# Earlier squares of x, square root for the norm factors, and three moved steps in a one-core encoder layer

## The chip, the cores and the metric

The kernel runs on one core of one Trainium2 chip. The core's engines are TensorE (PE, matmuls; PEld its weight loads), VectorE (DVE), ScalarE (ACT), GpSimd (POOL) and SyncE (SP, which issues most of the transfers). The metric is the device time of one execution in microseconds. Three executions of the kernel before took 2711.42 to 2716.16 us, with a median of 2714.16.

## The reference

One layer of a hybrid encoder for 512 tokens of width 2048, in float32:

```python
h = rmsnorm(x, mix_norm)
proj = h @ w_mix_in                       # 2048 -> 4*1024 + 16 + 3*1024
y_gdn = gdn_group(proj, ...)              # 8 heads x 128: gated delta rule
y_sc = shortconv_group(proj, ...)         # gated short convolution
x = x + concat(y_gdn, y_sc) @ w_mix_out
x = x + memory_xattn(rmsnorm(x), rmsnorm(mem), w_q, w_k, w_v, w_o)   # 256 memory tokens, 4 heads
x = x + conv_ffn(rmsnorm(x), w_ffn_up, ffn_conv, w_ffn_down)         # 2048 -> 2*5632 -> 2048
return rmsnorm(x, final_norm)
```

An `rmsnorm` multiplies each token by the reciprocal square root of the mean of its squares. The gates of the delta rule (`b_raw`, `a_raw`) are 16 columns of the input projection. Within a chunk the delta rule solves a unit lower triangular system per head, which the kernel does by inverting diagonal blocks of 32 x 32.

## The kernel before, in words

Activations lie with features on the 128 partitions and tokens along the row, so x is 16 tiles of 128 x 512. Each float32 weight piece (128 x 1024, 512 KB) is loaded by `wpiece` (line 136, tile `wst`, five buffers), rounded by ACT to `whi`, and the rest `wlo` is taken by DVE (lines 146 and 147). Both have three buffers, so the splits run up to three pieces ahead of PE.

The stages follow one another:

1. `values` (line 340): v of the memory tokens, before any norm of x is there. Eight column pairs n2 = 0 to 7; for each, 2 x 2 pieces go through `proj`, and `mem_out` (line 329) takes the result from PSUM by ACT and DVE (`kt`, `kth`; lines 332 to 337). The pairs 0 to 2 are held until `mem_norm` (after pair 2), so six `mem_out` calls come together then, and two after each later pair.
2. Beside it x is prepared. `load_x` loads tiles of x (SP, line 381), `square_x` calls `add_squares` (lines 260 to 264): ACT squares a tile into a tile `sq`, POOL adds it to `xacc`. `rstd_rows` (line 250) sums `xacc` over the partitions by a matmul with ones (`psn`, line 255), and `rsqrt` (line 228) makes the factor: Ln and Exp with scale -0.5 on ACT, then one Newton step on DVE (lines 241 to 243). `norm_x` (line 394) then scales the tiles of x by that factor and the gain. `beside_values` says behind which pair each of these stands.
3. A stage that folds v into the output weights (`psmo`, lines 634 to 636); in it x's operands for the input projection are made, and the 16 gate columns (`wba`, loaded at line 409) are multiplied with x (line 426).
4. The input projection with seven block products per quad (`quad_left`, `quad_right`; tiles `px`, `py`, `pz`).
5. The memory's keys (`psk`, line 1015), their fold into the queries' weights (`pswk`, lines 1032 to 1036) and the first half of the output rows (`out_row`, tile `psx1`). Into this PE work the delta rule is woven: generators `prepare_chunk`, `invert`, `solve`, `recur`, `scaled` for two groups of four heads (hb = 0, 1). `place` and `tick` count a clock of PE work in the code; a generator that has yielded (cost, wait) goes on when that clock has passed its wait. `invert` (lines 866, 867) is the substitution: 31 dependent steps of two DVE operations each, with a yield after each fourth. `solve` (line 876) then brings the inverted blocks (`xd`) and `v` back from DRAM and starts with transposes on PE. The last generator stores the heads' result to `y_d` (line 982), which the second half of the output rows reads.
6. Scores, softmax and the attention's output rows (`psx2`): `x1` is loaded from `x1_d` (line 1182), the product is added (line 1183), squares go to `acc2` by `add_squares`, and the sum is transposed for later (line 1159). `out_piece` loads and splits the next weights.
7. The feed-forward part: up projection with quads as in 4 (the norm's factor `r2` is made beside the first of them, by `norm_rows`), convolution, gate, down projection, final norm.

What sets the order: on PE the order is written out by hand in the stages under `manual_schedule`. On the other engines and queues a planner places the instructions when the program is built; it goes by program order among what is ready, and gives a tile its buffer when one of its tag is free. All tiles of the pool `tp` (64 buffers of 128 x 512, made by `T`) have one tag `t`: x, sq, kt, kth and the temporaries of `rsqrt` are among them. The pool `tb` of stages 3 and 6 has eight buffers. Every queue runs its instructions in the order that the planner gave them.

Of the kernel before, what the change touches and what calls it, by code (L numbers as in the profile page):

```python
# [69 lines left out]
def trunk(ctx: ExitStack, tc: tile.TileContext, g):  # L70
    nc = tc.nc
# [156 lines left out]
    def rsqrt(ms, ps, scale, bias):  # L228

        n = ms.shape[1]  # L230

        def tmp(s2):
            if n >= 256:
                return T(s2)[:, :n]
            return sp.tile([P, n], F32, tag=f"rs{n}{s2}", name=nm(s2))

        y = tmp("rsy")
        nc.scalar.activation(y, ps, AF.Ln, scale=scale, bias=bias)
        nc.scalar.activation(y, y, AF.Exp, scale=-0.5)
        t = tmp("rst")  # L240
        nc.vector.tensor_tensor(t, y, y, op=ALU.mult)
        nc.vector.scalar_tensor_tensor(t, t, -0.5, ms, op0=ALU.mult, op1=ALU.mult)
        nc.vector.scalar_tensor_tensor(y, t, 1.5, y, op0=ALU.add, op1=ALU.mult)
        return y
# [95 lines left out]
    def values(w, beside):  # L340

        out, held = [], []
        for n2 in range(KT // 2):
# [10 lines left out]
            else:  # L354
                ps = []
                for q in range(2):
                    ps.append((PG if n2 != 2 else PM)("psk"))
                    got = None
                    if n2 == 1:
                        got = ready[2 * q : 2 * q + 2]  # L360
                        got += [wpiece(w[3, 1])] if q else []
                    proj(lambda i: w[2 * n2 + q, i], mws, ps[q], ready=got)
# [35 lines left out]

    def beside_values(n2):
        if n2 == 0:  # L400
            return
        if n2 == 1:
            load_x(4)
        elif n2 < 5:
            load_x({2: 6, 3: 6, 4: 0}[n2])
            square_x(*((0, 4), (4, 10), (10, 16))[n2 - 2])
        elif n2 == 5:
            nc.vector.memset(wba, 0.0)
            nc.sync.dma_start(wba[:, :, 0:NG], g["w_ba"])
            r0.append(rstd_rows([xacc]))  # L410
        else:
            norm_x(4 * (n2 - 6), 4 * (n2 - 5))

    with tc.manual_schedule(engines={mybir.EngineType.PE}):
        vts = values(g["w_xv"], beside_values)
# [432 lines left out]
    def invert(hb):  # L848
# [13 lines left out]
        for m in range(B - 1):  # L862
# [5 lines left out]
            if m % 4 == 3:  # L868
                yield 0, 5.5, 0
# [6 lines left out]
    def solve(hb, j):  # L876
        i = hb, j
        xd = T("xd")[:, : 4 * B].rearrange("p (j r) -> p j r", j=4)
# [6 lines left out]
        v = vv[i] = load4("v", 2, hb, j)  # L885
# [281 lines left out]
    with tc.manual_schedule(engines={mybir.EngineType.PE}):  # L1167
        for idx in range(KT):
            n = order2[idx]
            if idx + 1 < KT:  # L1170
# [10 lines left out]
            x1 = TB("x2")  # L1181
            nc.sync.dma_start(x1, x1_d[n])
# [443 lines left out]
```

## Time and profile before

| what | value |
|---|---|
| median of three runs | 2714.16 us (2711.42 to 2716.16) |
| profiled execution, its own time | 2714.73 us |
| span of the profiled execution | 2712.6 us |
| PE busy | 2659.8 us (98%) |
| DVE busy | 2280.0 us (84%) |
| ACT busy | 1580.1 us (58%) |
| POOL busy | 311.9 us (11%) |
| mean granted clock of PE | 0.993 |
| HBM read, written | 472.83 MB, 67.39 MB |

How to read the rows shown below. A waits row is engine, operation and line, then what it waited for, then the sum in us, the number of times, and the longest. A timeline row is the start in us, the time taken, engine, line, operation, out<-in, shape and count; a bracket behind it is the idle time of the engine just before, and what ended it. A windows row is the stretch, its length, then busy time and instructions in brackets of PE, PEld, DVE, ACT and POOL, then the granted clock of PE (1.00 is full), the share of the DMA engines and GB/s. A groups row is line, engine, operation, tiles and count, then the sum in us, the mean of one in ns, and the idle time ahead of it. SPq rows are issues of transfers: the time is that of the issue, not of the transfer.

### The profile page before, as it was taken

The page shows a single profiled execution, that of the slowest core. Times are in us where ns is not written, and L with a number is a line of the kernel's source. Part 1 is how long each engine was busy: PE and PEld are TensorE (multiplying, and loading weights), DVE is VectorE, ACT ScalarE, POOL GpSimd, SP SyncE. Part 2 cuts the span into 40 slices and gives each one's busy share as a digit, 9 for nine tenths or more (in the row PEclk, how much of TensorE's full clock was granted, in tenths as well). Part 3 has the DMA queues.
Part 4 walks back from the last instruction along what each step waited for, and adds up shares of the span by engine and source line. Part 5 has one row for each costly group of instructions (what it writes and reads, how often), then busy time and mean ns, then how long its engine had stood idle before and what let it go on. Part 6 is the DMA issues. An engine that isn't in the chain of part 4 may idle for free.

```text
span 2712.6 us, 40226 instructions
## 1 busy us (share of the span) xinstructions
PE 2659.8 (98%) x14749; PEld 2294.4 (85%) x14749; DVE 2280.0 (84%) x3323; ACT 1580.1 (58%) x2301; POOL 311.9 (11%) x289
## 2 busy tenths in 40 slices
PE   9699999999999999999999999999999999999998
PEld 8578888888888998888778888888888888888886
DVE  7777777989899875466679999999999999878888
ACT  6575555656565675435666565656565655454545
POOL 1300000000010122030120000000000000000201
PEclk9899999999999999999999999999999999999999
DMA  8487667677776976665556767676767676864986
GB/s 269 152 273 217 172 162 186 177 189 186 193 222 202 290 238 202 236 195 185 167 151 185 194 175 194 177 196 173 200 175 198 170 196 201 257 194 142 280 251 182
DMA packets 264455, 542.86 MB, mean 200 GB/s; under 512 B 31665, under 2 KB 126529, under 8 KB 264257
## 3 DMA queue, kind: packets, MB, share of 16 engines
q1 hardware_dynamic: 192512, 400.53, 45.6%
q0 software_dynamic: 26912, 87.58, 18.7%
q10 hardware_dynamic: 44832, 52.18, 5.4%
q8 instruction: 115, 1.88, 0.3%
q14 instruction: 84, 0.68, 0.1%
HBM read 472.83 MB, written 67.39 MB: 199 GB/s over the span
## 4 chain that ended last, share of the span: by engine, by line
PE 85%; DVE 7%; DMA 3%; ACT 2%; issue 2%; SPq 0%; POOL 0%; ACTq 0%; DVEq 0%; POOLq 0%
PE px L172 19%; PE px L175 10%; PE pz L172 10%; PE pz L175 5%; PE py L172 5%; PE psd L1429 4%; PE psd L1427 4%; PE psd L1428 4%; PE psx L158 3%; PE psx L157 3%; PE psx L159 3%; PE py L175 2%; DVE wlo L147 1%; PE psk L172 1%; PE psmo L634 1%
## 5 line engine op out<-in xcount | busy, mean ns | idle before, releaser
L172 PE MATMUL px<-xo,whi 128*128 128x512 f32 x2288 | 573.8, 393 | 1.4 <-DVE ub L570 1.4
L475 ACT CAST whi<-wst 128x1024 fp32r<-128x1024 f32 x290 | 304.6, 1052 | 332.2 <-PE pz L172 195.6
L172 PEld LDWEIGHTS px<-xo,whi 128*128 128x128 f32 x2288 | 411.8, 189 | 76.0 <-DVE ub L570 1.6
L476 DVE TENSOR_TENSOR wlo<-wst,whi 128x1024 fp32r<-128x1024 f32 x290 | 353.6, 1220 | 22.1 <-ACT whi L475 22.1
L175 PEld LDWEIGHTS px<-xo,wlo 128*128 128x128 f32 x2288 | 312.2, 191 | 22.3
L147 DVE TENSOR_TENSOR wlo<-wst,whi 128x1024 fp32r<-128x1024 f32 x204 | 258.6, 1271 | 81.0 <-ACT whi L146 80.0
L146 ACT CAST whi<-wst 128x1024 fp32r<-128x1024 f32 x204 | 213.3, 1049 | 183.7 <-issue 62.9
L175 PE MATMUL px<-xo,wlo 128*128 128x256 f32 x2288 | 319.1, 282 | 0.0
L475 ACT CAST whi<-s 128x1024 fp32r<-128x1024 f32 x214 | 223.1, 1043 | 158.7 <-DVE wlo L476 83.8
L172 PE MATMUL pz<-xo,whi 128*128 128x512 f32 x1152 | 289.0, 393 | 0.5 <-ACT whi L475 0.5
L476 DVE TENSOR_TENSOR wlo<-s,whi 128x1024 fp32r<-128x1024 f32 x214 | 261.1, 1221 | 2.1 <-ACT whi L475 1.9
L1429 PE MATMUL psd<-wlo,hdh 128*128 128x512 f32 x616 | 240.7, 391 | 2.1 <-DVE wlo L1228 2.1
L1427 PE MATMUL psd<-whi,hdh 128*128 128x512 f32 x616 | 240.0, 390 | 0.1
L1428 PE MATMUL psd<-whi,hdl 128*128 128x512 f32 x616 | 239.8, 389 | 0.0
L172 PEld LDWEIGHTS pz<-xo,whi 128*128 128x128 f32 x1152 | 207.1, 189 | 37.6 <-ACT whi L475 0.9
L1225 ACT CAST whi<-wst 128x1024 fp32r<-128x1024 f32 x99 | 104.3, 1053 | 121.4 <-issue 53.2
L175 PEld LDWEIGHTS pz<-xo,wlo 128*128 128x128 f32 x1152 | 157.2, 191 | 11.2
L175 PE MATMUL pz<-xo,wlo 128*128 128x256 f32 x1152 | 160.6, 282 | 0.0
L1429 PEld LDWEIGHTS psd<-wlo,hdh 128*128 128x128 f32 x616 | 115.6, 188 | 29.4 <-DVE wlo L1228 5.3
L172 PE MATMUL py<-xo,whi 128*128 128x512 f32 x560 | 140.2, 392 | 0.0
L1228 DVE TENSOR_TENSOR wlo<-wst,whi 128x1024 fp32r<-128x1024 f32 x99 | 121.1, 1223 | 20.2 <-ACT whi L1225 17.9
L1428 PEld LDWEIGHTS psd<-whi,hdl 128*128 128x128 f32 x616 | 115.6, 188 | 24.1
(365 smaller groups left out, 5161.4 us busy)
## 6 DMA issues: line engine op xcount, KB each, us to landing
wst<-in_w_up SPq DMA_DIRECT2D x132, 512.0 KB, 4.2
wst<-in_w_dn SPq DMA_DIRECT2D x121, 512.0 KB, 4.6
s<-in_w_up POOLq DMA_DIRECT2D x87, 512.0 KB, 5.7
wst<-in_w_mix SPq DMA_DIRECT2D x84, 512.0 KB, 5.5
s<-in_w_mix POOLq DMA_DIRECT2D x55, 512.0 KB, 6.5
s<-in_w_up SPq DMA_DIRECT2D x43, 512.0 KB, 4.5
hid<-hf_d SPq DMA_DIRECT2D x77, 256.0 KB, 5.0
wst<-in_w_xo SPq DMA_DIRECT2D x32, 512.0 KB, 4.8
```

The lines of the kernel that those rows point to most:

```text
L146: nc.scalar.copy(hi, st)
L147: nc.vector.tensor_tensor(lo, st, f(hi), op=ALU.subtract)
L157: nc.tensor.matmul(ps, wh, xh, start=first, stop=False)
L172: nc.tensor.matmul(ps, hi[:, k * P : (k + 1) * P], x, start=first and k == 0, stop=False, skip_group_check=True)
L175: nc.tensor.matmul(ps[:, n:], lo[:, k * P : (k + 1) * P], x[:, :n], start=False, stop=end, skip_group_check=True)
L475: nc.scalar.copy(hi, t)
L476: tt(lo, t, f(hi), op=ALU.subtract)
L1225: nc.scalar.copy(hi[:, i * n : (i + 1) * n], t)
L1228: tt(lo[:, sl], t, f(hi)[:, sl], op=ALU.subtract)
L1427: nc.tensor.matmul(ps, xh, wh, start=first, stop=False)
L1428: nc.tensor.matmul(ps, xl, wh, start=False, stop=False)
L1429: nc.tensor.matmul(ps, xh, wl, start=False, stop=last)
```

## The change

Six edits:

- `rsqrt`: Ln and Exp on ACT are replaced by Sqrt on ACT and a reciprocal on DVE. The Newton step stays. It is called four times: for the memory (256 wide), for x (512), for the attention (4) and for the feed-forward part (512).
- Stage 1: x's loads were 4 behind pair 1, 6 behind pair 2, 6 behind pair 3; they are now 4 behind pair 1, 2 ahead of each of the four pieces of pair 2, 1 ahead of each piece of pair 3. The squares were 4 behind pair 2, 6 behind pair 3, 6 behind pair 4; they are now 2 ahead of each piece of pairs 3 and 4. `values` takes a second function, `beside_piece`, for that.
- The clearing of `wba` moves from behind pair 5 to behind pair 1, the load of the gates' weights into it from behind pair 5 to behind pair 4.
- `invert`: the wait in the yield after every fourth step is 7.0 instead of 5.5.
- `solve`: the load of `v` stands first, ahead of that of `xd`; it stood behind the product that makes `pt`.
- Stage 6: the load of `x1` stands at the head of the loop, ahead of `out_piece`; it stood behind the row's products.

```diff
--- before.py
+++ after.py
@@ -235,8 +235,8 @@
             return sp.tile([P, n], F32, tag=f"rs{n}{s2}", name=nm(s2))
 
         y = tmp("rsy")
-        nc.scalar.activation(y, ps, AF.Ln, scale=scale, bias=bias)
-        nc.scalar.activation(y, y, AF.Exp, scale=-0.5)
+        nc.scalar.activation(y, ps, AF.Sqrt, scale=scale, bias=bias)
+        nc.vector.reciprocal(y, y)
         t = tmp("rst")
         nc.vector.tensor_tensor(t, y, y, op=ALU.mult)
         nc.vector.scalar_tensor_tensor(t, t, -0.5, ms, op0=ALU.mult, op1=ALU.mult)
@@ -337,7 +337,7 @@
         nc.vector.tensor_tensor(th[:, NMEM:], t, f(th)[:, :NMEM], op=ALU.subtract)
         return th
 
-    def values(w, beside):
+    def values(w, beside, beside_piece):
 
         out, held = [], []
         for n2 in range(KT // 2):
@@ -359,7 +359,12 @@
                     if n2 == 1:
                         got = ready[2 * q : 2 * q + 2]
                         got += [wpiece(w[3, 1])] if q else []
-                    proj(lambda i: w[2 * n2 + q, i], mws, ps[q], ready=got)
+
+                    def weights(i):
+                        beside_piece(n2, 2 * q + i)
+                        return w[2 * n2 + q, i]
+
+                    proj(weights, mws, ps[q], ready=got)
             held.append(ps)
             if n2 < 2:
                 beside(n2)
@@ -396,23 +401,26 @@
     NG = 2 * H
     wba = T("wba").rearrange("p (k n) -> p k n", k=KT)
 
+    def beside_piece(n2, n):
+        if n2 in (2, 3):
+            load_x(2 if n2 == 2 else 1)
+        if n2 in (3, 4):
+            i = 8 * (n2 - 3) + 2 * n
+            square_x(i, i + 2)
+
     def beside_values(n2):
-        if n2 == 0:
-            return
         if n2 == 1:
+            nc.vector.memset(wba, 0.0)
             load_x(4)
-        elif n2 < 5:
-            load_x({2: 6, 3: 6, 4: 0}[n2])
-            square_x(*((0, 4), (4, 10), (10, 16))[n2 - 2])
+        elif n2 == 4:
+            nc.sync.dma_start(wba[:, :, 0:NG], g["w_ba"])
         elif n2 == 5:
-            nc.vector.memset(wba, 0.0)
-            nc.sync.dma_start(wba[:, :, 0:NG], g["w_ba"])
             r0.append(rstd_rows([xacc]))
-        else:
+        elif n2 > 5:
             norm_x(4 * (n2 - 6), 4 * (n2 - 5))
 
     with tc.manual_schedule(engines={mybir.EngineType.PE}):
-        vts = values(g["w_xv"], beside_values)
+        vts = values(g["w_xv"], beside_values, beside_piece)
 
     nc.vector.tensor_copy(mk[:, 0, 0:1], f(vts[0])[:, 0:1])
     nc.sync.dma_start(mk, g["masks"])
@@ -866,7 +874,7 @@
             nc.vector.tensor_tensor(t, am, x[:, :n, m : m + 1].broadcast_to([P, n, r]), op=ALU.mult)
             nc.vector.tensor_tensor(x[:, :n, m + 1 :], x[:, :n, m + 1 :], t, op=ALU.subtract)
             if m % 4 == 3:
-                yield 0, 5.5, 0
+                yield 0, 7.0, 0
         nc.sync.dma_start(xd_d[hb].rearrange("j n b (g c) r -> (j n b g) c r", g=G), x)
         for j in range(4):
             weave(solve(hb, j), 4.0 + 8.0 * j)
@@ -875,6 +883,7 @@
 
     def solve(hb, j):
         i = hb, j
+        v = vv[i] = load4("v", 2, hb, j)
         xd = T("xd")[:, : 4 * B].rearrange("p (j r) -> p j r", j=4)
         nc.sync.dma_start(xd, xd_d[hb][j].rearrange("n b c r -> (b c) n r"))
         yield 0, 5.0, 0
@@ -882,7 +891,6 @@
         p_ = v4(pt[i])
         blk = mk[:, M_BLK, :].rearrange("p (b c) -> p b c", c=B).unsqueeze(1).broadcast_to([P, 4, NB, B])
         nc.vector.tensor_tensor(p_.rearrange("p j (b c) -> p j b c", c=B), xd.unsqueeze(2).broadcast_to([P, 4, NB, B]), blk, op=ALU.mult)
-        v = vv[i] = load4("v", 2, hb, j)
         yield 0, 8.0
         psa = PG("psa")
         turn4(psa, pt[i])
@@ -1167,6 +1175,8 @@
     with tc.manual_schedule(engines={mybir.EngineType.PE}):
         for idx in range(KT):
             n = order2[idx]
+            x1 = TB("x2")
+            nc.sync.dma_start(x1, x1_d[n])
             if idx + 1 < KT:
                 out_piece()
             if idx == KT - 2:
@@ -1178,8 +1188,6 @@
             if idx == KT - 1:
                 begin_parts(first)
             ps = x2s[-1]
-            x1 = TB("x2")
-            nc.sync.dma_start(x1, x1_d[n])
             nc.vector.tensor_tensor(x1, ps, x1, op=ALU.add)
             turned.append((n, x1))
             add_squares(acc2, x1, idx == 0)
```

## The prediction

> **What bounds the kernel now.** I read the busy row of TensorE (PE) first, then PE's waits by releaser, then the timelines around the waits that the change touches.
>
> ```profile
> PE 2659.8 (98%) x14749; PEld 2294.4 (85%) x14749; DVE 2280.0 (84%) x3323; ACT 1580.1 (58%) x2301; POOL 311.9 (11%) x289
> ...
> PE psn L255 <- POOL xacc L264: 17.8, 1, 17.8
> PE pswk L1036 <- DVE wlo L147: 4.4, 3, 1.8
> PE psmo L635 <- DVE wlo L147: 2.1, 1, 2.1
> PE psxt L1159 <- DVE x L1183: 2.1, 1, 2.1
> PE psvt L788 <- DMA v<-qkvz_d: 2.0, 1, 2.0
> ```
>
> PE is busy for 2659.8 of 2712.6 us, and the change takes no matmul away. So all it can win lies in 52.8 us of idle time and in time run at a lower clock. One wait is a third of that: the column sum of x's squares (psn, line 255) waits 17.8 us for the adds on POOL. What a wait costs beside its length is seen in the granted clock just behind it:
>
> ```profile
> 96.00:98.00 2.00, 2.00 (x4) 1.01 (x3) 0.56 (x1) 0.00 (x0) 0.00 (x0) 0.50 0.70 66
> 98.00:100.00 2.00, 2.00 (x7) 1.56 (x6) 0.13 (x1) 1.78 (x2) 0.00 (x0) 0.67 0.00 0
> 932.00:936.00 4.00, 4.00 (x22) 4.00 (x22) 3.25 (x11) 2.29 (x4) 0.00 (x0) 0.57 1.09 390
> ```
>
> The column behind POOL is the clock. After the long wait it is 0.50 and 0.67 for two times 2 us, 1.7 us lost; after the wait of 2.0 us on line 788 it is 0.57 over 4 us, again 1.7 us. So a wait of 2 us costs about 3.7, and a long one that only gets shorter keeps its 1.7.
>
> **Part 1: x's loads and squares.** ACT squares a tile (sq), POOL adds it to xacc; the order on ACT:
>
> ```profile
> 28.71 0.64 ACT L260 ACTIVATE xacc<-x 128x512 f32<-128x512 f32 x1 [0.91 <-DMA x<-in_x]
> ...
> 46.98 0.35 ACT L332 COPY kt<-psk 128x256 f32<-128x256 f32 x1
> ...
> 63.62 0.40 ACT L336 CAST kth<-kt 128x256 fp32r<-128x256 f32 x1
> 66.41 1.67 ACT L263 ACTIVATE sq<-x 128x512 f32<-128x512 f32 x3
> ...
> 77.58 3.22 ACT L263 ACTIVATE sq<-x 128x512 f32<-128x512 f32 x6
> ...
> 86.23 3.22 ACT L263 ACTIVATE sq<-x 128x512 f32<-128x512 f32 x6
> ```
>
> The first square needs no tile of the pool "t" and runs at 28.71, as its x lands. The next three have their x (the first four loads went out together) and still run at 66.41, behind the six mem_out copies of pairs 0 to 2 (46.98 to 63.62). I read this as tiles of one tag being given out in program order: sq gets its buffer after those six kt and kth. The change moves the squares into the pieces of pairs 3 and 4, but the six mem_outs (after pair 2) still stand ahead of them. So the first add can't start at 30 us; it starts about when the last kth is placed, 63.62, plus one square (1.67/3 = 0.56): 64.2 instead of 67.11. What ends the wait is POOL:
>
> ```profile
> 67.11 5.53 POOL L264 TENSOR_TENSOR xacc<-xacc,sq 128x512 f32<-128x512 f32 x3 [31.15 <-ACT sq L263]
> 78.35 16.92 POOL L264 TENSOR_TENSOR xacc<-xacc,sq 128x512 f32<-128x512 f32 x12 [5.70 <-ACT sq L263]
> ...
> 95.32 2.07 PE L255 MATMUL psn<-xacc,ones 128*128 128x512 f32 x2 [17.83 <-POOL xacc L264]
> ```
>
> An add takes 5.53/3 = 1.84 us while the split of weights fills DVE, and 16.92/12 = 1.41 us while PE stands still. PE comes free at 95.32 - 17.83 = 77.5. From 64.2 to 77.5 POOL does 7 adds at 1.84; the other 8 at 1.41 end at 77.5 + 11.3 = 88.5 or so, as seven squares stand together now instead of three, which closes the gap of 5.70. The wait falls from 17.8 to about 11: **6.8 us gained**. If all adds took 1.41 it would end at 85.4 (9.9 gained), if all took 1.84, at 91.8 (3.5). The clock's 1.7 us stay, as 11 us are still a long wait.
>
> The twelve x loads and the gates' weights now go out together ahead of pair 3's pieces on SP. That is eight loads more at 1.92/4 = 0.48 us of issue:
>
> ```profile
> 23.30 1.92 SPq L381 DMA_DIRECT2D x<-in_x  x4
> 28.13 23.90 SPq L143 DMA_DIRECT2D wst<-in_w_xv  x10
> ...
> 36.61 1.05 ACT L146 CAST whi<-wst 128x1024 fp32r<-128x1024 f32 x1 [1.74 <-PE psk L172]
> ...
> 94.71 0.66 SPq L409 DMA_DIRECT2D wba<-in_w_ba  x1
> ```
>
> Issue reaches 23.30 + 12 x 0.48 + 0.66 = 29.7, so pair 3's first piece leaves 1.6 us later than 28.13. Its cast is at 36.61, and PE wants it behind 42.9, three pieces on. I take nothing for it, with 0 to 3 us for a piece that lands behind twelve times 256 KB of x. The clearing of wba (0.48 us on DVE) leaves the stretch after the wait: that is worth nothing, as the gates' matmuls come a stage later.
>
> Behind psn DVE stays as it was, only earlier: eight scalings of x at a time and the splits, with PE's wait of 2.1 (psmo) in it. As the mem_outs of pair 5 now fall behind psn, I add **1.0 us** (from -2 to +4).
>
> **Part 2: square root and reciprocal for Ln and Exp.** Per call one table load and Exp on ACT go, one reciprocal on DVE comes. DVE sits before rst in all of them:
>
> ```profile
> 47.11 0.42 DVE L241 TENSOR_TENSOR rst<-rsy 128x256 f32<-128x256 f32 x1 [2.27 <-ACT rsy L239]
> 102.16 0.69 DVE L241 TENSOR_TENSOR rst<-rsy 128x512 f32<-128x512 f32 x1 [4.04 <-ACT rsy L239]
> 1430.55 1.22 DVE L552 TENSOR_TENSOR s<-s,wst 128x1024 f32<-128x1024 f32 x1
> 1433.14 0.69 DVE L241 TENSOR_TENSOR rst<-rsy 128x512 f32<-128x512 f32 x1 [1.37 <-ACT rsy L239]
> 1434.49 1.88 PE L172 MATMUL px<-xo,whi 128*128 128x512 f32 x7 [1.43 <-DVE ub L570]
> ...
> L824 DVE RECIPROCAL bk<-ss 128x4 f32<-128x4 f32 x8 | 1.3, 168 | 0.0
> L666 DVE RECIPROCAL beta<-beta 128x32 f32<-128x32 f32 x1 | 0.3, 347 | 0.0
> ```
>
> No wide reciprocal is in the trace. Low bound: 0.69 us for 512, the other 128x512 rows of DVE. High bound, from the slope (347 - 168)/28 = 6.4 ns per element: 347 + 480 x 6.4 = 3.4 us, and 1.8 for 256. I take 3.4, as the slope is the row of the operation itself. At 47 and 102 DVE's empty 2.27 and 4.04 us hide it. At 1433 the cover is 1.37: the sum ub, for which PE already waits 1.43, comes some 2 us later, and a wait of 3.4 draws the clock's 1.7: **3.5 us lost**; -1.4 if it is cheap (that wait goes), +4.8 if the planner also puts the 1.22 us of line 552 between reciprocal and ub.
>
> [...]
>
> **Part 3: v sooner in solve.**
>
> ```profile
> 919.05 0.66 SPq L879 DMA_DIRECT2D xd<-xd_d  x1
> 925.70 0.37 SPq L795 DMA_DIRECT2D v<-qkvz_d  x1
> ...
> 931.93 0.86 PE L788 MATMUL psvt<-mk,v 128*128 128x128 f32 x4 [1.96 <-DMA v<-qkvz_d]
> ```
>
> The v that PE waits for is issued 6.7 us after its xd, on SP, as its tile comes after that of pt, which waits for xd. Now it goes out ahead of xd, which leaves 0.4 us later for it. PE's wait of 1.96 with its 1.7 of clock goes: **3.7 us gained** (0 if PE then waits for pt in its place).
>
> **Part 4: gaps of 7.0 for 5.5.** Seven gaps per head group put off what follows the substitution by 7 x 1.5 = 10.5 in the code's clock. DVE is what it relieves:
>
> ```profile
> 860.00:872.00 12.00, 10.10 (x62) 8.68 (x60) 11.93 (x29) 6.37 (x13) 0.06 (x1) 1.00 0.91 283
> 872.60 0.39 PE L1036 MATMUL pswk<-kth,wlo 128*128 128x256 f32 x1 [1.84 <-DVE wlo L147]
> 979.45 0.39 PE L1036 MATMUL pswk<-kth,wlo 128*128 128x256 f32 x1 [1.73 <-DVE wlo L147]
> ...
> 1108.11 0.37 SPq L982 DMA_DIRECT2D y_d<-so  x1
> 1132.93 0.69 DVE L153 TENSOR_TENSOR ypl<-yg,yph 128x512 fp32r<-128x512 f32 x1 [2.02 <-ACT yph L152]
> ...
> DMA to landing us min/median/max: 2.3/3.2/7.0
> DMA to landing us min/median/max: 3.6/4.7/7.0
> ```
>
> DVE is full (11.93 of 12 us), and two splits late by 1.84 and 1.73 us cost 7 us with the clock. A gap takes no work from DVE, it only lets later splits go first; new collisions are as likely. I take **1.5 us gained**, from 7 gained to 4 lost. The two landing rows are those of the stores to y_d and of the loads from it. The later chain ends its last store's issue at 1108.11 + about 11 = 1119, ahead of the last split of y at 1132.93, so nothing for that.
>
> **Part 5: x1's load ahead of out_piece.** Its tile of the pool "tb" comes in the same turn as before, and on SP it only passes one load of mo_d, which is issued a piece ahead; so I take 0; at best the wait of 2.1 us on line 1159 goes with its clock (-3.8).
>
> **Sum**, against the profiled execution's own 2714.7 (span 2712.6 and 2.1 around it; the median is 2714.2): -6.8 + 1.0 + 3.5 - 3.7 - 1.5 = -7.5, so **2707.2 us**.
>
> **Rivals.**
> - *The long wait closes.* If buffers are not given out in program order, the squares follow the loads and POOL ends before 77.5. Then 17.8 + 1.7 go instead of 6.8: 2707.2 - 12.7 = 2694.5. For it: ACT has idle time from 30 us on. Against: the three squares that had their x and waited until 66.41.
> - *Nothing to measure.* POOL takes 1.84 throughout (3.5 gained), the reciprocal costs 4.8, gaps shift waits without removing any, v's wait alone goes: 2714.7 - 3.5 + 1.0 + 4.8 - 3.7 = 2713.3. For it: DVE is at 84% and gets two wide reciprocals. Against: the closed gap of 5.70 us on POOL.
> - *Slower: y comes late.* The second half of the output rows starts behind the split at 1132.93 and takes the heads in turn, 0.69 apart by the code's cost, so it wants head 4, the first of the second group, some 3 us on. A store lands in 3.2, a load in 4.7, and cast and split take about 1.3. So it decides once the last store of y leaves after 1132.9 + 3 - 9.2 = 1126.7, 18.6 us later than now; from there each us is one of PE. The gaps give 11; if the first head group's delay also held up the second's substitution, 22, and with DVE as full as above perhaps 34. Then it costs 15.4 and 1.7 of clock: 2707.2 + 17.1 = 2724.3. Against: the second substitution starts from its own preparation, not from the first.
>
> **How the numbers follow.** Forecast 0.58, closed wait 0.13, nothing to measure 0.21, late y 0.08. A change under 0.2% (5.4 us) can't be told from none here, so faster means below 2708.7 and slower above 2719.6. The forecast's own range is 2700 to 2714 by its unknown terms, of which I put 0.42 on the faster side and 0.16 within. With the closed wait that makes 0.55 faster, with the second rival 0.37 within, and 0.08 slower. The range from 2697 to 2716.5 leaves out the closed wait and the late y, 0.2 in all, and holds the rest with the bounds of the reciprocal, the gaps and the adds.
>
> **What would show it.** Right: psn's wait at 8 to 14 us and its first add near 64; squares in two groups of seven and eight; a 128x512 reciprocal near 3.4 us; a longer wait for ub after 1430; none for v. Wrong: squares before 60 us (my reading of the order falls), a wide reciprocal under 1 us, or new waits over 2 us between 840 and 1135.

## The result, and the profile after

| | before | after |
|---|---|---|
| median | 2713.63 us of 4 runs (2711.42 to 2716.16) | 2739.19 us of 4 runs (2736.20 to 2739.47) |
| ratio to before, 95% interval | | 1.0091 [1.0074, 1.0109] |
| profiled execution, its span | 2714.73, 2712.6 us | 2739.47, 2737.6 us |

The change makes the kernel 25.6 us slower. The forecast was 2707.2, and the range ended at 2716.5, so both are wrong. The line numbers of the profile after are higher by 8 behind the first stage (line 950 is now 958, 1036 is 1044, 982 is 990).

The busy row of the page after, and then PE's waits (engine, line, what it waited for; sum, times, longest):

```profile
PE 2666.7 (97%) x14749; PEld 2297.1 (84%) x14749; DVE 2290.3 (84%) x3327; ACT 1577.2 (58%) x2294; POOL 303.7 (11%) x289
```

```profile
PE psn L255 <- POOL xacc L264: 13.9, 1, 13.9
PE psmo L643 <- DVE wlo L147: 6.4, 1, 6.4
...
PE psx L157 <- ACT yph L152: 3.7, 1, 3.7
PE psk L175 <- DVE wlo L147: 3.6, 1, 3.6
PE pso L958 <- issue: 3.6, 1, 3.6
PE pso L958 <- DVE vn L949: 3.3, 1, 3.3
PE psk L172 <- DVE kt L334: 2.6, 1, 2.6
```

PE does the same 14749 matmuls. The wait for the squares has shrunk from 17.8 to 13.9 and the wait for v is gone. But six waits of 2.6 to 6.4 us stand in the list that were not there or were at most 2.1: two behind the squares (psmo, psk for splits), one at the memory's pieces (kt), two in the delta rule (pso), one at the output rows (yph). The two of pso are what the prediction named as a sign that it is wrong, new waits of over 2 us between 840 and 1135.

The squares of the kernel after, as POOL adds them:

```profile
67.37 11.67 POOL L264 TENSOR_TENSOR xacc<-xacc,sq 128x512 f32<-128x512 f32 x7 [31.47 <-ACT sq L263]
81.63 12.50 POOL L264 TENSOR_TENSOR xacc<-xacc,sq 128x512 f32<-128x512 f32 x8 [2.59 <-ACT sq L263]
```

They run in groups of seven and eight, and the gap on POOL between them is 2.59 instead of 5.70. The wide reciprocals, in the groups of the kernel after (sum, then the mean of one in ns):

```profile
L239 DVE RECIPROCAL rsy<-rsy 128x512 f32<-128x512 f32 x2 | 6.7, 3344 | 0.0
L239 DVE RECIPROCAL rsy<-rsy 128x256 f32<-128x256 f32 x1 | 1.8, 1753 | 0.5 <-ACT rsy L238 0.5
```

They take 3.34 and 1.75 us, as estimated (3.4 and 1.8). The stores of the output rows, by their line, of before and of after (the last two numbers are the starts of the first and the last):

```profile
L982 SPq DMA_DIRECT2D y_d<-so x8: 359/370/377, 974.6 to 1108.1; - x8
```

```profile
L990 SPq DMA_DIRECT2D y_d<-so x8: 359/370/378, 1004.3 to 1144.0; - x8
```

The last one comes 35.9 us later; the prediction had 11. The three stretches of the delta rule and the output rows, of before and then of after (width; busy time of PE, PEld, DVE, ACT, POOL; granted clock; DMA share; GB/s):

```profile
870.00:990.00 120.00, 112.78 (x1034) 108.94 (x1033) 107.16 (x223) 82.94 (x148) 27.47 (x15) 0.96 0.84 262
990.00:1110.00 120.00, 119.56 (x888) 104.83 (x887) 62.17 (x82) 69.87 (x97) 30.48 (x21) 1.00 0.69 221
1110.00:1240.00 130.00, 130.00 (x575) 107.63 (x575) 79.34 (x73) 49.21 (x67) 26.05 (x15) 1.00 0.64 206
```

```profile
870.00:990.00 120.00, 108.58 (x983) 103.01 (x981) 104.92 (x219) 74.22 (x136) 18.91 (x12) 0.96 0.86 266
990.00:1110.00 120.00, 115.06 (x888) 102.51 (x888) 68.17 (x96) 69.40 (x98) 31.11 (x22) 0.97 0.65 194
1110.00:1240.00 130.00, 125.51 (x556) 103.36 (x556) 68.23 (x71) 51.65 (x67) 20.05 (x15) 0.99 0.62 204
```

Idle time of PE is the width less the first busy time; to it comes the width times what the clock lacks of 1.00. Before, that is 12.0, 0.4 and 0 us in the three stretches; after, it is 16.2, 8.5 and 5.8, which is 18 us more in all (the clock has two digits, so each number may be off by 0.6).

The same loss is seen from outside in the start of the first matmul of each stage, taken from the rows of its line (us from the span's start):

| first matmul of | before | after | gap alone | v alone | squares alone | root alone | squares on DVE |
|---|---|---|---|---|---|---|---|
| psn of x (L255) | 95.3 | 94.2 | 95.0 | 95.0 | 91.0 | 97.7 | 83.3 |
| gates (psba) | 132.2 | 138.8 | 130.3 | 130.3 | 135.9 | 136.2 | 122.3 |
| memory's key weights (pswk, L1032) | 870.4 | 878.9 | 869.2 | 870.1 | 873.2 | 874.9 | 862.5 |
| attention's scores | 1221.1 | 1248.0 | 1232.8 | 1221.1 | 1225.2 | 1225.3 | 1214.3 |
| last projection (psd) | 2278.2 | 2303.2 | 2288.1 | 2276.0 | 2280.1 | 2281.4 | 2270.7 |
| span | 2712.6 | 2737.6 | 2724.5 | 2710.6 | 2715.3 | 2715.5 | 2705.4 |

So of the 25.0 us, 6.6 are lost up to the gates, 1.9 from there to the key weights, and 18.4 between the key weights and the scores (26.9 at the scores less 8.5); behind that 1.9 come back. The columns to the right belong to the experiments. The six kernels that are alike up to the gates (before, gap alone, v alone, residual rows alone, and the two with a gap of 4.0) start them at 130.3 to 132.2, so a difference of less than 2 us in that row tells nothing.

### The profile page after: what moved, and what is told of

Its sections match the earlier page's. It is cut to its first block, busy times and chain, and to the rows that moved or that the text cites. A ratio compares the mean times of both kernels' runs of the same rounds, so it can differ in the third digit from the quotient of the medians.

```text
span 2737.6 us, 40229 instructions
## 1 busy us (share of the span) xinstructions
PE 2666.7 (97%) x14749; PEld 2297.1 (84%) x14749; DVE 2290.3 (84%) x3327; ACT 1577.2 (58%) x2294; POOL 303.7 (11%) x289
## 4 chain that ended last, share of the span: by engine, by line
PE 85%; DVE 7%; DMA 3%; issue 2%; ACT 2%; POOL 1%; SPq 0%; ACTq 0%; DVEq 0%; POOLq 0%
PE px L172 19%; PE px L175 10%; PE pz L172 9%; PE pz L175 5%; PE py L172 5%; PE psd L1437 4%; PE psd L1435 4%; PE psd L1436 4%; PE psx L158 3%; PE psx L157 3%; PE psx L159 3%; PE py L175 2%; PE psk L172 2%; DVE wlo L147 1%; PE psmo L642 1%
## 5 line engine op out<-in xcount | busy, mean ns | idle before, releaser
L175 PEld LDWEIGHTS pz<-xo,wlo 128*128 128x128 f32 x1152 | 157.2, 190 | 11.3
```

The costliest lines, as they stand in the source:

```text
L175: nc.tensor.matmul(ps[:, n:], lo[:, k * P : (k + 1) * P], x[:, :n], start=False, stop=end, skip_group_check=True)
```

## The experiments

Theory A said that the gap is the cause, B that v's tile is, C that the squares cost behind psn what they win ahead of it. Each kernel is the one before with the edit shown, but for one, which starts from the kernel after.

| kernel | median us | before, same chip | ratio, 95% interval |
|---|---|---|---|
| gap 7.0 alone | 2728.05 | 2713.07 | 1.0060 [1.0043, 1.0076] |
| v alone | 2715.56 | 2713.07 | 1.0009 [0.9999, 1.0018] |
| squares and gates' weights alone | 2717.25 | 2713.07 | 1.0017 [1.0008, 1.0027] |
| square root and reciprocal alone | 2718.06 | 2713.07 | 1.0016 [1.0006, 1.0025] |
| residual rows (x1) alone | 2713.79 | 2712.82 | 1.0004 [0.9995, 1.0013] |
| after, with gap 5.5 | 2726.44 | 2712.82 | 1.0047 [1.0031, 1.0064] |
| gap 4.0 | 2726.49 | 2712.82 | 1.0047 [1.0032, 1.0062] |
| gap 4.0 and v | 2723.04 | 2713.30 | 1.0043 [1.0028, 1.0058] |
| squares in the third pair | 2710.20 | 2712.82 | 0.9989 [0.9979, 0.9998] |
| the same, adds on DVE | 2706.86 | 2713.30 | 0.9977 [0.9967, 0.9986] |
| the change's squares, adds on DVE | 2707.16 | 2713.30 | 0.9975 [0.9965, 0.9984] |
| three pairs, adds on DVE | 2709.02 | 2714.62 | 0.9976 [0.9967, 0.9985] |

The five single parts cost 15.0, 2.5, 4.2, 5.0 and 1.0 us by their medians, 27.6 together, against 25.6 for the whole: the parts add up, and none of them wins (those of v and of the residual rows can't be told from nothing).

### The gap alone

```diff
             if m % 4 == 3:
-                yield 0, 5.5, 0
+                yield 0, 7.0, 0
```

> The kernel before with part 4 alone (7.0 for 5.5). Theory A (the wider gaps put the second head group's chain into the output rows, and its last store of y late): 14 to 20 us slower than before, the last store of y near 1140 instead of 1108, and the loss all behind 1019, where the output rows begin. Theory B (it is v's earlier tile, which takes a buffer of the tag in its turn, that puts off the chain): within 4 us of before, the last store of y near 1119.

Measured 2728.05, 15.0 more. The stores of the output rows, and the three stretches, of this kernel:

```profile
L982 SPq DMA_DIRECT2D y_d<-so x8: 359/370/378, 994.0 to 1131.7; - x8
```

```profile
870.00:990.00 120.00, 109.55 (x1012) 104.97 (x1011) 104.86 (x217) 77.94 (x141) 17.51 (x13) 0.97 0.82 262
990.00:1110.00 120.00, 115.88 (x862) 101.96 (x861) 59.86 (x79) 65.32 (x92) 29.40 (x21) 0.97 0.66 201
1110.00:1240.00 130.00, 127.82 (x560) 104.61 (x559) 74.91 (x75) 55.08 (x73) 23.13 (x17) 1.00 0.63 206
```

The first store comes 19.4 us later and the last one 23.6, so each of the two head groups is late by about 20. But the gaps themselves make less than half of that. The substitution ends with the store of the inverted blocks to `xd_d`, once in each group (the last two numbers are these two starts), in the kernel before and in this one:

```profile
L870 SPq DMA_DIRECT2D xd_d<-xb x2: 326/326/327, 891.7 to 982.0; - x2
```

```profile
L870 SPq DMA_DIRECT2D xd_d<-xb x2: 319/323/327, 900.5 to 986.7; - x2
```

It ends 8.8 and 4.7 us later. From their first steps on (843.1 and 930.8 before, 841.8 and 929.3 here) the two substitutions have become 10.0 and 6.2 us longer, near the 10.5 of the code's clock or under it. The rest of the delay arises behind them, in `solve`, `recur` and `scaled`: the first product of the recurrence (pv) comes 14.2 us later in the first group and 7.8 in the second, and the first product of the second group's second chunk (pr) 21.4 later (1061.0 for 1039.6). Why the chain slips so far there was not tried. Counted as above, the three stretches lose 2.0, 7.3 and 2.2 us. Only the last of them are waits for output rows. The 7.3 between 990 and 1110 come from the delta rule's own last chunks, which now stand so late that PE meets them before their inputs are made; the two waits there, from PE's timeline:

```profile
1024.86 0.50 PE L975 MATMUL psn<-snh,onesr 128*128 128x512 f32 x1 [1.72 <-ACT bt L890]
1044.05 2.08 PE L950 MATMUL pso<-dt,vn 128*128 128x128 f32 x8 [2.39 <-DVE vn L941]
```

Behind the second one the eight matmuls take 2.08 us, where eight took 1.16 in the kernel before (at 1034.28): the granted clock between 1044 and 1048 is 0.50. Theory A holds, and most of the loss lies ahead of the reader of the output rows.

### After, with the gap at 5.5

```diff
-                yield 0, 7.0, 0
+                yield 0, 5.5, 0
```

> The changed kernel with the substitution's gap back at 5.5; the other four parts stay. Theory A (the gap's loss stands by itself, as in the run of the gap alone, +15): the last output row is stored at about 1120 instead of 1144, the waits for output rows after 1150 go, and the time is 2739 - 15 = 2724, range 2720 to 2728; some 11 above the kernel before stay, from squares, square root and v. Rival: the gap's loss overlaps with the lateness of the others (the rows are late already because the first stage ends later): then less than 8 comes back, 2731 or more.

Measured 2726.44: by the medians 12.8 come back, the last store stands at 1117.1, and the first matmul of the scores at 1230.1, 17.9 earlier than in the kernel after. Theory A holds: the gap's loss stands by itself.

### A gap of 4.0, without and with v's move

```diff
-                yield 0, 5.5, 0
+                yield 0, 4.0, 0
```

> The kernel before with a gap of 4.0 instead of 5.5 in the substitution. Theory A1 (a gap is pure delay of the output rows, the same 10 us per unit either way): the last output row is stored at about 1085, and 2713 - 15 = 2698. Theory A2 (at 5.5 the rows are just in time for their reader at 1115 to 1150, so an earlier row gives nothing): last row at 1085 to 1100, time 2711 to 2715. Rival A3 (the steps of the substitution get in the way of VectorE's splits when they stand closer): waits for splits (wlo) between 1020 and 1100 grow, 2717 or more.

Measured 2726.49. A1 and A2 fall: a shorter gap loses as much as a longer one. A3 has the right sign and the wrong place, since no wait for a split grows between 1020 and 1100. The first stretch of this kernel, and the longest wait of PE in it:

```profile
870.00:990.00 120.00, 104.62 (x931) 99.95 (x932) 101.40 (x208) 73.32 (x134) 25.27 (x15) 0.90 0.73 223
```

```profile
939.25 1.08 PE L788 MATMUL psvt<-mk,v 128*128 128x128 f32 x4 [4.10 <-DMA v<-qkvz_d]
```

The loss is at the other end of the delta rule now: PE idles 15.4 of these 120 us instead of 7.2, and the clock falls to 0.90. The shorter gap has also won little: the two substitutions are only 2.6 and 3.5 us shorter, where the code's clock has 10.5, and the second one starts 10.2 later (941.0). The v that PE waits for leaves 0.8 us before PE comes to it (934.4 against 939.25 - 4.10 = 935.15), where it was 4.3 ahead in the kernel before (925.7 against 930.0); its pt, behind which it stands in the code, is made at 931.5 instead of 924.7. The next kernel loads v at the start of solve, beside the gap of 4.0.

> The kernel before with the gap at 4.0 and v loaded at the start of a solve. Theory A3' (at 4.0 the loss came from 870 to 960, where TensorE waited 4.1 for v and then ran 3 to 4 us at a low clock; v's load stood too late because the steps in front of it stand closer): the wait of 4.1 goes, the granted clock of 930 to 960 returns to 0.94 or more, and 5 to 8 of the 13 come back: 2718 to 2721. Rival A4 (the loss is spread over the chain's small waits, v's being one of several that take each other's place): less than 3 comes back, 2723 to 2727.

Measured 2723.04; 3.4 us come back. The same two views of this kernel:

```profile
870.00:990.00 120.00, 105.40 (x974) 101.47 (x975) 103.16 (x212) 76.87 (x139) 26.32 (x15) 0.96 0.79 240
```

```profile
937.17 0.54 PE L909 MATMUL ps<-pt,ww 32*32 32x32 f32 x13 [3.65 <-ACT ww L904]
```

The wait for v is gone and the clock is back at 0.96 (between 930 and 960, where A3' looked, at 0.94 from 0.83), as A3' said. But PE still idles 14.6 us: in place of v it waits 3.65 for the copy ww of the very same chain. What comes back lies between the two theories, and by the time A4 is nearer. I read this as a chain whose steps stand too close and which waits for its own last step, whichever of its waits that is; two kernels don't prove it.

### v alone

```diff
     def solve(hb, j):
         i = hb, j
+        v = vv[i] = load4("v", 2, hb, j)
...
-        v = vv[i] = load4("v", 2, hb, j)
```

> The kernel before with part 3 alone (v ahead of xd). Theory A: no slower than before, PE's wait of 1.96 us for v gone, 2 to 4 us faster in the best case. Theory B: 14 to 20 us slower, the last store of y some 25 us later.

Measured 2715.56, which can't be told from before. Theory B falls as the cause of the loss, and so does the gain that the prediction took. The wait of 1.96 for v is gone, and this is what stands on PE's timeline in that place:

```profile
910.70 1.16 PE L784 MATMUL pskq<-q,k 128*128 128x128 f32 x8 [1.50 <-DVE dt L839]
926.51 0.62 PE L909 MATMUL ps<-pt,ww 32*32 32x32 f32 x13 [1.30 <-ACT ww L904]
```

The first of the three stretches of this kernel says what became of the gain:

```profile
870.00:990.00 120.00, 108.68 (x1032) 104.09 (x1031) 107.64 (x221) 83.10 (x148) 26.04 (x15) 1.00 0.82 261
```

The clock is 1.00 instead of 0.96, which is worth 4.8 us, but PE idles 11.3 us instead of 7.2. It also shows that a wait of about 2 us doesn't always cost 3.7. In the kernel before, the clock fell behind the wait of 1.84 at 872.60 (0.77 and 0.80 over the next two times 4 us); behind the same wait here, of 1.85, it stayed at 1.00.

### Square root and reciprocal alone

```diff
-        nc.scalar.activation(y, ps, AF.Ln, scale=scale, bias=bias)
-        nc.scalar.activation(y, y, AF.Exp, scale=-0.5)
+        nc.scalar.activation(y, ps, AF.Sqrt, scale=scale, bias=bias)
+        nc.vector.reciprocal(y, y)
```

> The kernel before with part 2 alone (square root and reciprocal). Theory A: two wide reciprocals of 3.35 us and one of 1.75 stand on DVE, the first gate matmul comes 4 to 7 us later than 132.2, the time 4 to 8 us over before. Theory C: first gate matmul within 2 us of 132.2, time within 3 us of before.

Measured 2718.06, 5.0 more. DVE's and PE's rows around the memory's norm, PE's wait before the gates, and PE at the norm of the feed-forward part:

```profile
44.90 1.75 DVE L239 RECIPROCAL rsy<-rsy 128x256 f32<-128x256 f32 x1 [0.54 <-ACT rsy L238]
51.10 0.42 DVE L334 TENSOR_TENSOR kt<-psk,kt 128x256 f32<-128x256 f32 x1
```

```profile
51.67 2.06 PE L172 MATMUL psk<-mw,whi 128*128 128x512 f32 x8 [2.58 <-DVE kt L334]
...
129.19 0.63 PE L635 MATMUL psmo<-wlo,kth 128*128 128x512 f32 x1 [3.86 <-DVE wlo L147]
...
1435.01 2.00 PE L172 MATMUL px<-xo,whi 128*128 128x512 f32 x8
...
1437.78 1.42 PE L172 MATMUL px<-xo,whi 128*128 128x512 f32 x5 [0.31 <-DVE ub L570]
```

The reciprocal fits DVE's empty time ahead of the norm, and yet kt, the first reading of a psk buffer, starts at 51.10 instead of 47.45: two splits and one more step of the norm now stand between the norm's reciprocal and it on DVE. PE, which wants that buffer, waits 2.58. The gates start 4.0 us later. At 1433, where the prediction put its whole loss, the start of the last projection is only 3.2 later than before, less than the 4.0 that were lost already: nothing more goes there. The reciprocal of 3.35 us does delay ub, but PE's order in this part is the planner's too, and it has put ten other matmuls (eight px at 1435.01, then two py) ahead of the one that needs ub. The wait for ub is 0.31 here; before it was 1.43.

### The residual rows alone

```diff
             n = order2[idx]
+            x1 = TB("x2")
+            nc.sync.dma_start(x1, x1_d[n])
             if idx + 1 < KT:
...
-            x1 = TB("x2")
-            nc.sync.dma_start(x1, x1_d[n])
```

> The kernel before with only the early load of the residual rows in the projection's loop. Theory A: the load is hidden anyway, its issue moves by one place, 0 to -2 us: 2711 to 2713.5. Rival: SP's queue holds the two weight loads of the projection's next piece back behind the row's load, and PE gets the small waits of the end: 2715 or more.

Measured 2713.79, 1.0 more, and the interval of the ratio holds 1: no change that can be told.

### The squares alone

The edit is the change's own in values, beside_piece and beside_values; the rest stays as before. The clearing and the load of the gates' weights moved with it and weren't tried by themselves.

> The kernel before with part 1 alone (loads and squares of x, gates' weights). Theory A (the loss of the first stage comes from the reciprocal on DVE): the wait for the sum of x's squares falls from 17.8 to about 12 us, the first gate matmul comes 2 to 6 us sooner than 132.2, the time 2 to 6 us under before. Theory C (POOL's adds now run beside PE's splits on DVE and slow those, so the loss is the squares' own): first gate matmul at 134 or later, time 2 us or more over before.

Measured 2717.25. psn starts at 91.0, 4.3 us earlier; the gates start 3.7 later. PE's waits behind psn, and DVE at 84 us:

```profile
117.33 2.08 PE L175 MATMUL psk<-mw,wlo 128*128 128x256 f32 x8 [4.60 <-DVE wlo L147]
128.87 0.79 PE L643 MATMUL psmo<-wlo,kth 128*128 128x512 f32 x1 [5.43 <-DVE wlo L147]
```

```profile
83.98 4.49 DVE L147 TENSOR_TENSOR wlo<-wst,whi 128x1024 fp32r<-128x1024 f32 x2
```

Two splits take 4.49 us beside POOL's adds, 2.25 each; alone one takes 1.22. Theory C holds so far. Whether POOL's adds do it, or the place, the next four kernels tell.

### The squares in the third pair

```diff
+    def beside_piece(n2, n):
+        if n2 == 2:
+            load_x(3)
+            square_x(4 * n, 4 * n + 4)
...
-        elif n2 < 5:
-            load_x({2: 6, 3: 6, 4: 0}[n2])
-            square_x(*((0, 4), (4, 10), (10, 16))[n2 - 2])
```

> The kernel before with x loaded and squared during the third pair already, so that all 16 squares stand in program order ahead of the mean square of the memory and of the six pieces held for it; gap, logarithm and exponential, v and the residual rows as before. Theory C1 (what set the start of the squares was their place behind the six held pieces): GpSimd's adds run from about 37 to 60, the wait of 17.8 for the sum of squares goes, the ones-matmul of the norm starts at 78 to 80, the clock does not drop there, and the time is 2713 - 15 = 2698, range 2694 to 2703. Theory C2 (GpSimd beside VectorE costs VectorE's splits what it gives): the wait goes too, but TensorE waits for splits (3 to 6 each) between 36 and 60 and between 100 and 135; the first px matmul comes less than 6 earlier, 2707 to 2715. Rival C3: the x loads crowd out the weights of the third pair, TensorE waits for them at 33 to 45, 2710 or slower.

Measured 2710.20. POOL's row, then DVE's groups in the stretch from 44 to 62 (sum, mean of one in ns, idle time ahead), then PE's longest waits:

```profile
35.45 27.08 POOL L264 TENSOR_TENSOR xacc<-xacc,sq 128x512 f32<-128x512 f32 x15
```

```profile
L147 DVE TENSOR_TENSOR wlo<-wst,whi 128x1024 fp32r<-128x1024 f32 x4 | 8.5, 2137 | 2.9 <-ACT whi L146 2.9
...
L337 DVE TENSOR_TENSOR kth<-kt,kth 128x256 fp32r<-128x256 f32 x1 | 1.5, 1477 | 0.0
...
L334 DVE TENSOR_TENSOR kt<-psk,kt 128x256 f32<-128x256 f32 x1 | 0.4, 409 | 0.0
```

```profile
63.29 3.75 PE L172 MATMUL psk<-mw,whi 128*128 128x512 f32 x8 [4.23 <-DVE mk L422]
...
120.87 0.80 PE L640 MATMUL psmo<-wlo,kth 128*128 128x512 f32 x1 [5.58 <-DVE wlo L147]
```

The reading that the place in program order sets the start is shown to be right: put ahead of the six held pieces, the adds start at 35.45, as soon as POOL is through with the memory's, and the wait for psn is gone. Whether the buffers of the tag do it, or the planner's order alone, this kernel doesn't tell. But the gates start only 4.5 us earlier, where C1 had 15 in all: four waits of 2.6 to 5.6 stand where one of 17.8 and two of about 2 stood. That is C2, though only the two behind 100 are for splits; the two early ones are for the memory's pieces (kt, mk). C3 falls, there is no wait before 49.

The rows say what a POOL add costs DVE. An operation with both inputs in SBUF loses up to 1.1 us, a long one no more than a short one: the split goes from 1.22 to a mean of 2.14 in this stretch (2.30 at most), the 256-wide kth from 0.42 to 1.48. It doesn't lose that every time: two earlier splits beside the same adds, at 37.5 and 40.0, took 1.34 and 1.23. An operation of the same length with one input in PSUM (kt<-psk,kt) keeps its 0.41. There is one of these here, and 13 more stand beside POOL's adds in the kernels before, after and with the squares alone, each at 0.41 or 0.42. A copy with its only input in SBUF isn't spared (rmem<-rsy, 0.25 to 0.84). The losses run from 0.0 to 1.1 us, and what makes them was not shown.

### The same, with the adds on DVE

```diff
-            nc.gpsimd.tensor_tensor(acc, acc, sq, op=ALU.add)
+            (eng or nc.gpsimd).tensor_tensor(acc, acc, sq, op=ALU.add)
...
-            add_squares(xacc, xts[i], i == 0)
+            add_squares(xacc, xts[i], i == 0, nc.vector)
```

> The early squares again, their 15 adds moved from GpSimd to VectorE. Theory C2 (beside a GpSimd add, VectorE's 256-wide operations took 1.4 to 1.6 instead of 0.42 and a split 2.0 to 2.3 instead of 1.22, so GpSimd's 27 us of adds cost VectorE more than the 15 x 0.69 = 10 us that it needs to add itself): the 256-wide operations stay at 0.42, the waits of 2.6 and 4.2 at 49 and 59 shrink to at most 3 together, the norm's ones-matmul starts at 78 to 82 instead of 88.4, the first psba matmul at 118 to 122, and the time is 2710 - 7 = 2703, range 2699 to 2707. Rival C4 (VectorE is simply full between 37 and 66; who adds doesn't matter): splits of the third pair come late, TensorE waits at 36 to 46 as long as before at 49 to 59, ones-matmul at 86 or later, 2709 or more.

Measured 2706.86, at the edge of what C2 gave. DVE's row of three adds in a line, and PE's longest wait:

```profile
47.67 2.28 DVE L264 TENSOR_TENSOR xacc<-xacc,sq 128x512 f32<-128x512 f32 x3
```

```profile
55.52 3.75 PE L172 MATMUL psk<-mw,whi 128*128 128x512 f32 x8 [6.46 <-DVE kt L334]
```

An add takes 0.76 us in this row. The slow 256-wide operations are gone (0.41 to 0.43 each from 46 to 58, a copy 0.24), but the wait for kt is 6.46 in one piece where it was 2.58 and 4.23, and psn starts at 86.2, not at 78 to 82. So the two expectations share it: DVE is full in this place (busy for 10.86 of the 12 us from 42 to 54), and who adds seems to matter by some 3 us besides (0.9977 against 0.9989, whose intervals overlap).

### The change's squares, with the adds on DVE

The edit is that of the squares alone and the one just shown together.

> The change's own part on the squares (spread over the fourth and fifth pair, weights of the gates earlier), alone, with the 15 adds on VectorE instead of GpSimd. Theory C2: the splits stay at 1.22 in 66 to 95, the adds end with the last square at about 84 to 86 instead of 91, TensorE's waits for splits at 117 and 129 (4.6 and 5.4) go to 1 to 2 each, the first psba matmul comes at 126 to 129 instead of 135.9, and the time is 2717 - 8 = 2709, range 2705 to 2712. Rival: the two late splits come from the norm's 16 products standing in front of them, whoever adds the squares: then the waits stay at 4 to 5 and the time at 2714 or more.

Measured 2707.16, against 2717.25 with the adds on POOL in the same place. DVE's row of a split between the adds, and PE's waits:

```profile
80.48 1.22 DVE L147 TENSOR_TENSOR wlo<-wst,whi 128x1024 fp32r<-128x1024 f32 x1
```

```profile
83.29 2.07 PE L255 MATMUL psn<-xacc,ones 128*128 128x512 f32 x2 [5.62 <-DVE xacc L264]
104.00 1.94 PE L175 MATMUL psk<-mw,wlo 128*128 128x256 f32 x8 [4.75 <-DVE wlo L147]
116.88 0.50 PE L643 MATMUL psmo<-wlo,kth 128*128 128x512 f32 x1 [1.53 <-DVE wlo L147]
```

One edit, the engine of 15 adds, is worth 10 us. The split takes 1.22, as alone. The wait for psn falls from 13.94 to 5.62 and that for psmo from 5.43 to 1.53; only the one for psk stays (4.75 against 4.60), so the rival was right in that one. The gates start at 122.3 instead of 135.9. Of these 13.6 us, 7.7 are there at psn already, as the adds end sooner; the other 5.9 are won behind it. Some of it is given back by the scores (1214.3 against 1221.1 before).

### Three pairs, with the adds on DVE

The adds stand on DVE as just shown, and x's late loads in the third pair.

```diff
+        k = {2: (2, 2, 2, 0), 3: (2, 2, 2, 2), 4: (1, 1, 0, 0)}.get(n2)
+        if k:
+            square_x(done[0], done[0] + k[n])
+            done[0] += k[n]
```

> The kernel before with the 15 adds on VectorE and the squares spread over three pairs: 6 in the third (ahead of the mean square of the memory), 8 in the fourth, 2 in the fifth; the 12 late x loads during the third pair; gap, logarithm and exponential, v, gates' weights and residual rows as before. Theory C5 (VectorE's free time in 30 to 54, about 8 of 24, takes 4 us of adds without making the memory's pieces late, and the adds end before TensorE wants them): no wait for the sum of squares, ones-matmul at 77.5 to 79 instead of 83.3, first psba matmul at 118 to 121 instead of 122.3, time 2704 to 2706 against 2707.2 for the squares in two pairs on VectorE. Rival C6 (VectorE bounds the stretch from 40 to 126 as a whole; an add moved forward only moves the wait): a wait of 3 to 6 at 49 to 55, first psba matmul at 121 to 125, time 2706 to 2709.

Measured 2709.02 beside 2714.62, ratio 0.9976, the same as in two pairs (0.9975). PE's waits, and the fullest stretch:

```profile
82.67 1.13 PE L255 MATMUL psn<-xacc,ones 128*128 128x512 f32 x2 [2.86 <-DVE xacc L264]
108.28 2.08 PE L175 MATMUL psk<-mw,wlo 128*128 128x256 f32 x8 [4.10 <-DVE wlo L147]
119.14 0.80 PE L645 MATMUL psmo<-wlo,kth 128*128 128x512 f32 x1 [5.41 <-DVE wlo L147]
```

```profile
114.00:126.00 12.00, 6.86 (x18) 5.43 (x19) 11.46 (x22) 4.95 (x13) 0.00 (x0) 0.72 0.27 87
```

The wait for psn is shorter by 2.8 than with two pairs and that for psmo longer by 3.9, and DVE is busy for 11.46 of 12 us. That is C6 in the main: DVE bounds this stretch, and an add moved forward moves the wait. But the wait that C6 named at 49 to 55 isn't there (1.1 at most), and the gates start later than either theory had. The three kernels with the adds on DVE can't be told from one another (0.9975 to 0.9977), and all three beat both kernels. Why the gates start at 122.3 in one of them and at 127.4 in another, and the spans still agree within 0.1 us, was not settled.

## Why the prediction was wrong, by its own steps

**Gaps (part 4): this step failed.** It took 1.5 gained, from 7 gained to 4 lost, and a last store at 1119; alone the gap costs 15.0, and the last store stands at 1131.7. Three things in it were wrong. The 7 x 1.5 = 10.5 were about right for the substitution itself, which got 10.0 and 6.2 us longer, but "put off what follows" by as much was not: behind it the delay grew to 19.4 at the first store and 23.6 at the last. A chain goes on only at the places where a group of matmuls is issued, so it can slip by more than the gap; that this makes the rest is argued from the code and was not tried. "DVE is what it relieves": the waits for splits on line 1036 stayed (4.7 us in all, 4.4 before). And the lateness was watched at the reader of the output rows only, where it cost 2.2 of 11.5 us; most went where PE met the delta rule's own last chunks too early. The bound on the loss side, 4 us, was the estimate of two collisions, with no row behind it for a chain that has to fit its cover on both sides; as a gap of 4.0 costs 13.7 us and one of 7.0 costs 15.0, 5.5 was such a fit.

**The rival of the late y** had the sign and, by chance, nearly the price: 17.1 us against 15.0. (Its 3.2 us for a store to land is the median of the stores and the loads of y_d together; the eight stores alone land in 2.4 in the kernel before, the loads in 4.7.) Its line for a DVE "as full as above", 34 us later, is what the whole change did (35.9). Its mechanism, the reader waiting, is the smaller part, and its chance of 0.08 was too low.

**Squares (part 1): the step behind psn failed.** The start was right to the digit, 64.23 in the kernel with the squares alone against 64.2, and so was the reason, the place in program order, which the third-pair kernel showed by turning it round. The 15 adds took 24.2 us together, the sum that had been taken (1.67 and then 1.56 each for 1.84 and 1.41). The wait fell to 13.9 instead of 11 because POOL still stood idle for 2.59 us between the two groups, a gap that the step took as closed: 4.3 gained for 6.8, inside the bounds. (77.5 + 11.3 is 88.8 and not 88.5, a slip of 0.3, and the gates' weights left at 44.5, not with the twelve x loads; neither matters.) What failed is "Behind psn DVE stays as it was, only earlier", 1.0 lost with at most 4: from psn to the gates 8.0 us were lost (from 4.3 ahead to 3.7 behind). The step priced what DVE costs POOL, 1.84 for 1.41, and left out what POOL costs DVE: with the adds on DVE, in the same place, 2.1 are lost there (from 12.0 ahead to 9.9 ahead). In the whole kernel the first add slipped to 67.37, behind the memory's pieces, which the reciprocal had delayed.

**Square root (part 2).** The durations were right, 3.34 and 1.75 us for 3.4 and 1.8, as the slope of the rows had them. The sum was near too, 3.5 against 5.0 (2.9 by the spans), but by luck, as the place was wrong: "At 47 and 102 DVE's empty 2.27 and 4.04 us hide it" did not hold, as the splits that come due meanwhile then stand ahead of kt; and the loss of 3.5 at 1433 did not show, as PE had other matmuls to do there.

**v (part 3).** The wait went as said and the clock came back, but the 3.7 us did not come: 2.5 more, which can't be told from nothing. The bound "0 if PE then waits for pt in its place" was the case, with waits for vn, dt and ww as well as pt. And the 3.7 rested on "a wait of 2 us costs about 3.7", which the wait of 1.85 in that kernel doesn't bear out.

**x1 (part 5)** was right: nothing.

**Sum.** Of five terms, three had the wrong sign or size by 4 us and more (gaps 16.5, squares 10.0 off with what lies behind psn, v 6.2); and by the medians all five erred on the same side, while the range was made as if they erred apart. Even with every term at its bound on the losing side (3.3 for the adds, 3.0 behind psn, 1.3 for the reciprocal, 3.7 for v, 5.5 for the gaps) the sum ends at 2724.0, so the bounds of the gaps and of what lies behind psn were too narrow as well.

## What to carry to other kernels

Price an operation on GpSimd by what it takes from VectorE as well: beside it an operation with two inputs in SBUF lost up to 1.1 us, and 15 adds of 0.76 us were cheaper by 10 us on VectorE in the change's own place (2707.16 for 2717.25), though it was busy for 11.38 of the 12 us from 66 to 78 with them. A chain that is woven into other work fits on both sides: before a gap is changed, look for what waits if the chain is late and for what waits if it is early, and count the delay in stores seen, not in the code's clock: here the gaps came out at or under their length, and the chain behind them lost as much again or more. Idle time ahead of an instruction covers a longer one only if nothing else comes due on that engine meanwhile: a reciprocal of 1.75 us in 2.27 us of idle time still put kt off from 47.45 to 51.10.

## What the runs showed of the hardware

- A split of 128x1024 takes 1.22 us alone and 1.23 to 2.33 beside POOL's running adds (mean 2.14 in the stretch shown); 256-wide operations with two inputs in SBUF go from 0.42 to as much as 1.52, with one in PSUM they stay at 0.41 or 0.42 (14 of 14).
- POOL's add of 128x512 takes 1.81 us over the 15 in a row of the squares in the third pair (27.08), and 1.67 and 1.56 in the two groups of the kernel after; the same add on DVE takes 0.76 (2.28 for three).
- The reciprocal on DVE takes 3.34 us for 512 elements a partition and 1.75 for 256, which is 6.2 ns for each element more.
- A wait of PE of 1.7 to 2.0 us drew a lower clock three times in the kernel before (1.7 us lost behind each, at 872.60, 931.93 and 979.45); the wait of 1.90 at 113.27 in the same kernel (1.00 from 113 to 121) and one of 1.85 in the kernel with v alone drew none.
